# HGRN scores with the second half of the tokens reversed, so that keys of both halves share one stationary operand

## The chip, the core and the metric

The kernel runs on one core of a Trainium2 chip. The metric is the device time of one execution in microseconds (us). A core has a matrix engine (TensorE, PE in the rows, with PEld for its loads of the stationary operand), a vector engine (VectorE, DVE), an engine for activations and copies (ScalarE, ACT), GpSimd (POOL) and queues that start DMAs (SP for most). SBUF is the working memory with 128 partitions; PSUM takes the results of matmuls, in banks of 512 fp32 words per partition.

## The reference, cut to what matters

Four layers (HGRN2, mLSTM, S5, HGRN2), each followed by a SwiGLU block, over 256 tokens of width 1024. The change concerns the HGRN2 mixer of layers 0 and 3: 8 heads of 128 channels.

```python
q, f, v, g = split(x @ w_in, 4)
log_f = logaddexp(log(lb), log1p(-lb) + log_sigmoid(f))
k = (1 - lb) * sigmoid(-f);  q = silu(q)
# per head, with b = cumsum(log_f) along the tokens:
att[t, s] = sum_d q[t, d] * k[s, d] * exp(b[t, d] - b[s, d])     # for s <= t, else 0
o[t] = sum_s att[t, s] * v[s]
# the reference does this in chunks of 64 tokens with a carried state
o = rmsnorm_per_head(o) * silu(g);  return o @ w_out
```

The decay between key s and query t is a product of the gates of all tokens after s up to t, one for each channel.

## The kernel before

**Scores.** The 256 tokens are two halves of 128. Everything in the scores lies with the channels on the 128 partitions and the tokens along them. Heads are worked in pairs; a pair's keys `k`, gates `f` and queries `q` hold four blocks of 128 tokens in the order head 0 half 0, head 0 half 1, head 1 half 0, head 1 half 1. `hgrn_scores` builds `att` (keys on partitions, queries along) for a pair by doubling: at level m (1, 2, 4, ... 64) the queries in the right m of each 2m tokens meet the keys in the left m. Keys and queries are multiplied in place by products of gates, level by level (L604, L606), so that the product of a key and a query at level m already has its decay; `e` holds the products of gates of whole runs and is halved at each level (L613). The keys of half 0 with the queries of half 1 come last, as `cross` (L617).

**Matmuls of a pair.** The diagonal product (L574) streams 192 columns for each of the four blocks: 128 queries, and 64 queries already times their gate, which serve level 1. Identity and a mask pick the wanted entries into `att` (L576, L577). At levels 2 to 16 ACT gathers the left runs of keys and the right runs of queries of a block into one tile `kq` (L587, L588); PE takes all 128 columns of it as the stationary operand and streams its 64 queries (L590), one matmul for each block; a masked copy puts the result into `att` (L592). At levels 32 and 64 PE reads keys and queries directly, in blocks of m by m (L597), and ACT copies the result (L598).

**Order.** `scores` (L511) runs two pairs at once, level by level, and puts matmuls of other steps between (`query`, `pieces` of v and g, `heads_out`). The order on each engine is planned when the kernel is built: an instruction whose inputs are expected late is passed by a later one, but on the chip every engine keeps its planned order. Matmuls with weights are made of three fp32r products (`mm3`), with the weight in two parts that ACT (L123) and DVE (L124) make from each staged MB.

**Other names.** `pair_proj` (L467) makes gates or queries of one pair with 2 x 8 x 3 = 48 matmuls of 256 columns by `ws_block` (L157). `norm` and `put_split` (L198, L229) write the next layer's input, transposed, as two parts `xh` and `xl`; `head_turn` (L390) does that for the heads' output. The masks come from DRAM by one POOL DMA in each HGRN layer (L434).

```python
for i in range(4):                                        # L589, levels 2 to 16
    nc.tensor.matmul(pl[:, i * 64 : (i + 1) * 64], kq[:, i], split(kq, m)[:, i, :, 1], start=True, stop=True)
```

Of the kernel before, what the change touches and what calls it, by code (L numbers as in the profile page):

```python
# [28 lines left out]
LEVELS = (64, 32, 16, 8, 4, 2, 1)  # L29
# [5 lines left out]
class Trunk:  # L35
# [162 lines left out]
    def norm(self, h, banks, gb, last=None, perm=False):  # L198
# [18 lines left out]
        for n in range(4):  # L217
# [8 lines left out]
            self.put_split(pt[:, o : o + 256], 2 * n, h, perm=perm)  # L226
        self.x[h] = z

    def put_split(self, pt, k0, h, scale=None, perm=False, to=None):  # L229
# [3 lines left out]
        src = pt.rearrange("p (k t) -> p k t", k=n)  # L233
        t = slice(h * P, (h + 1) * P)
# [12 lines left out]
    def ffn(self, i, gb, out=None, perm=False, extra=()):  # L247
        nc, tc = self.nc, self.tc
        with tc.tile_pool(name=self.uid("ffn"), bufs=2, reuse_waits="tile") as fp:
# [112 lines left out]
            for h in range(2):  # L362
                self.layernorm(h, down[h], gb, out, perm)
# [26 lines left out]
    def head_turn(self, src, n, h, scale, ot):  # L390
# [4 lines left out]
        self.put_split(pt, 4 * n, h, scale, to=ot)  # L395
# [31 lines left out]
    def hgrn(self, j, gb, lb=None):  # L427
        nc, tc = self.nc, self.tc
        nw = self.const.tile([P, 1], F32, name=f"hnw{j}")
        nc.gpsimd.dma_start(nw, self.a["hg_nw"][j])  # L430
        with tc.tile_pool(name=self.uid("hg"), bufs=1, reuse_waits="tile") as hp, \
                tc.tile_pool(name=self.uid("hw"), bufs=2, reuse_waits="tile") as wp:
            msk = hp.tile([P, 5, 64], F32, name=self.uid("msk"))
# [33 lines left out]
            def pair_proj(st, tag="g"):  # L467
                us = self.wstage("w_hg", j, st)
                ps = self.bank(tag)
                for e in range(2):  # L470
                    self.ws_block(ps[:, e * 256 : (e + 1) * 256], us[e])
                return ps

            def heads_out(n):
# [3 lines left out]
                for h in range(2):  # L478
                    for e in range(4):
# [4 lines left out]
                        nc.tensor.matmul(o, att[:, 2 * (hd % 2) + h, :], v[:, h, c], start=True, stop=h == 0)  # L484
# [6 lines left out]
                for h in range(2):  # L491
                    on[n, h] = wp.tile([P, 768], F32, tag="q", name=self.uid("on"), bufs=4)[:, 0:512]
# [3 lines left out]
            def turn(n, h):  # L496
                o, gate = on[n, h], g[:, h, n * 512 : (n + 1) * 512]
                nc.vector.tensor_tensor(o, o, gate, ALU.mult)
                self.head_turn(o, n, h, nw, ot)
# [3 lines left out]
            def query(pr):  # L503
                pq = pair_proj(4 + pr, "a")
                q[pr] = wp.tile([P, 4, 192], F32, tag="q", name=self.uid("q"), bufs=4)
                self.act(q[pr][:, :, 0:P], pq.rearrange("p (a t) -> p a t", a=4), AF.Silu)
# [32 lines left out]
    def hgrn_gates(self, wp, pr, pf, lb):  # L539
# [11 lines left out]
        if lb is not None:  # L551
            for i in range(2):
                hd, s = slice(2 * pr + i, 2 * pr + i + 1), slice(i * 256, (i + 1) * 256)
                act(f[:, s], f[:, s], AF.Identity, scale=lb[:, 1, hd], bias=lb[:, 0, hd])
                act(k[:, s], k[:, s], AF.Copy, scale=lb[:, 1, hd])
        return k, f

    def hgrn_scores(self, wp, q, k, f, msk):
# [3 lines left out]

        nc = self.nc
        mul = lambda o, x, y: nc.vector.tensor_tensor(o, x, y, ALU.mult)
        att = wp.tile([P, 512], F32, tag="att", name=self.uid("att"), bufs=3).rearrange("p (a t) -> p a t", a=4)
        kt = k.rearrange("p (a t) -> p a t", a=4)
        qt = q[:, :, 0:P]
        e = f.rearrange("p (a n) -> p a n", a=4)
        split = lambda t, m: t.rearrange("p a (n s m) -> p a n s m", s=2, m=m)
# [9 lines left out]
        ends = wp.tile([P, 256], F32, tag="ends", name=self.uid("ends"))  # L579
        spare = 0  # L580
        for m in (1, 2, 4, 8, 16, 32, 64):
            n = P // (2 * m)
            if m > 1:
                pl = self.bank("a")
                if m < 32:
                    kq = wp.tile([P, 4, P], F32, tag="kq", name=self.uid("kq"))
                    nc.scalar.copy(split(kq, m)[:, :, :, 0], split(kt, m)[:, :, :, 0])  # L587
                    nc.scalar.copy(split(kq, m)[:, :, :, 1], split(qt, m)[:, :, :, 1])  # L588
                    for i in range(4):  # L589
                        nc.tensor.matmul(pl[:, i * 64 : (i + 1) * 64], kq[:, i], split(kq, m)[:, i, :, 1], start=True, stop=True)  # L590
                    mk = msk[:, 5 - m.bit_length(), :].bitcast(I32).rearrange("p (n m) -> p n m", m=m)
                    nc.vector.copy_predicated(split(att, m)[:, :, :, 1], mk[:, None].broadcast_to([P, 4, n, m]),  # L592
                                              pl[:, 0:256].rearrange("p (a n m) -> p a n m", a=4, m=m))
                else:
                    for lo in range(0, P, 2 * m):
                        for i in range(4):
                            nc.tensor.matmul(pl[lo : lo + m, i * m : (i + 1) * m], kt[:, i, lo : lo + m], qt[:, i, lo + m : lo + 2 * m], start=True, stop=True)  # L597
                        nc.scalar.copy(att[lo : lo + m, :, lo + m : lo + 2 * m], pl[lo : lo + m, 0 : 4 * m].rearrange("p (a t) -> p a t", a=4))  # L598
            ee = e.rearrange("p a (n s) -> p a n s", s=2)
            mine = slice(0, 4) if m < 64 else slice(0, 4, 2)  # L600
            his = slice(0, 4) if m < 64 else slice(1, 4, 2)
            b = lambda x, r: x[..., None].broadcast_to([P, len(range(4)[r]), n, m])
            x = split(kt, m)[:, mine, :, 0]
            mul(x, x, b(ee[:, mine, :, 1], mine))  # L604
            x = split(qt, m)[:, his, :, 1]
            mul(x, x, b(ee[:, his, :, 0], his))  # L606
            if m < 64:
                if m == 1:
                    new = ends
                else:  # L610
                    new, spare = f[:, spare : spare + 4 * n], spare + 4 * n
                e = new.rearrange("p (a n) -> p a n", a=4)
                mul(e, ee[:, :, :, 0], ee[:, :, :, 1])  # L613
            yield
        pc = self.bank("a")
        for i in range(2):
            nc.tensor.matmul(pc[:, i * P : (i + 1) * P], kt[:, 2 * i], qt[:, 2 * i + 1], start=True, stop=True)  # L617
        cross = wp.tile([P, 2, P], F32, tag="cross", name=self.uid("cross"), bufs=3)
        nc.scalar.copy(cross, pc[:, 0:256].rearrange("p (a t) -> p a t", a=2))
        yield att, cross  # L620
# [581 lines left out]
def trunk(tc, aps, out, layers=range(DEPTH), ffn=True):  # L1202
    with ExitStack() as ctx:
# [4 lines left out]
        perm0 = layers[0] == 2  # L1208
        with tc.tile_pool(name="first", bufs=1, reuse_waits="tile") as fp:
            src = fp.tile([P, KD, S], F32, name="xt")  # L1210
            t.warm_up(fp)
            for k in (slice(0, 2), slice(2, 4), slice(4, KD)):
                nc.sync.dma_start(src[:, k], aps["xt"][:, k])
                y, dh, dl = src[:, k], t.xh[:, k], t.xl[:, k]
                if perm0:
                    y = y.rearrange("p k (h c j) -> p k h j c", h=2, j=4)
                    dh, dl = (x.rearrange("p k (h j c) -> p k h j c", h=2, j=4) for x in (dh, dl))
                for h in (slice(0, 1), slice(1, 2)) if perm0 else (slice(0, S),):
# [127 lines left out]
```

## Time and profile before

| | before |
|---|---|
| median of 3 runs | 1317.61 us (1316.46 to 1317.88) |
| the profiled execution | 1319.75 us |
| its span, first to last instruction | 1317.9 us |
| PE busy | 1295.8 us, 98% |
| DVE busy | 968.3 us, 73% |
| ACT busy | 713.7 us, 54% |
| mean granted clock of PE | 0.994 |

A page of the profile gives busy times, the span in slices, the chain of work that ended last and groups of instructions by line. Views by window, by form, by line, of waits and in order of time go into it more closely. Records of matmuls overlap, and their ends are modelled, so the distance from one start to the next is a better measure than a record's duration. An fp32 matmul leaves two records, an fp32r one a single record. [...]

### The profile page before, as it was taken

The numbers are of one execution on the slowest core, as the hardware profiler recorded it, in microseconds if no ns is written. First come the engines' busy times: TensorE is split into PE (matmuls) and PEld (weight loads), VectorE is DVE, ScalarE is ACT, GpSimd is POOL, SyncE is SP. The second block draws the span as 40 slices with busy tenths as digits, with TensorE's granted clock in tenths as the row PEclk, the third lists the DMA queues.
The fourth block names the chain that finished last, engine by engine and source line by source line (L and its number), as shares of the span: only waits on it lengthen the run. The fifth ranks groups of instructions, "written<-read, shape, count | busy, mean of one in ns | idle before, by whom it ended". The sixth has DMA issues, their size and how long they took to land.

```text
span 1317.9 us, 19258 instructions
## 1 busy us (share of the span) xinstructions
PE 1295.8 (98%) x7430; PEld 1094.3 (83%) x7430; DVE 968.3 (73%) x1680; ACT 713.7 (54%) x1146; POOL 52.3 (4%) x75
## 2 busy tenths in 40 slices
PE   8999999999999999999998999999999999999997
PEld 6998888888788878888877778888879888888885
DVE  5877789776687699768489877666585886866664
ACT  5744475665556655657442355555459554555550
POOL 0000100000100110000010000000010001000001
PEclk8999999999999999999999999999999999999999
DMA  7732276657364257756567647555555312755540
GB/s 286 264 139 99 92 259 221 243 190 268 125 255 158 98 176 258 237 207 226 190 239 264 235 155 258 180 183 185 187 199 190 130 64 99 285 177 182 188 157 32
DMA packets 46123, 249.78 MB, mean 190 GB/s; under 512 B 5344, under 2 KB 9456, under 8 KB 19664
## 3 DMA queue, kind: packets, MB, share of 16 engines
q1 hardware_dynamic: 45712, 248.08, 52.7%
q8 instruction: 58, 0.95, 0.3%
q0 software_dynamic: 320, 0.48, 0.1%
q14 instruction: 33, 0.27, 0.1%
HBM read 234.91 MB, written 13.63 MB: 189 GB/s over the span
## 4 chain that ended last, share of the span: by engine, by line
PE 92%; DVE 3%; ACT 2%; DMA 1%; issue 1%; POOL 0%; SPq 0%; POOLq 0%; DVEq 0%; ACTq 0%
PE g L169 17%; PE g L140 10%; PE g L141 10%; PE g L142 10%; PE g L172 9%; PE a L140 8%; PE a L141 8%; PE a L142 8%; PE a L590 2%; PE t L1092 1%; PE t L224 1%; PE g L1080 1%; PE a L597 1%; PE a L574 1%; PE t L983 1%
## 5 line engine op out<-in xcount | busy, mean ns | idle before, releaser
L124 DVE TENSOR_TENSOR lo<-w,hi 128x1024 fp32r<-128x1024 f32 (+1 forms) x394 | 477.0, 1218 | 138.9 <-ACT hi L123 129.9
L123 ACT CAST hi<-w 128x1024 fp32r<-128x1024 f32 (+1 forms) x394 | 411.3, 1048 | 196.6 <-PE a L141 111.3
L169 PE MATMUL g<-xx,hi 128*128 128x512 f32 x1024 | 358.5, 395 | 0.2 <-DVE sum L301 0.2
L172 PE MATMUL g<-xx,lo 128*128 128x256 f32 x1024 | 267.4, 281 | 0.0
L169 PEld LDWEIGHTS g<-xx,hi 128*128 128x128 f32 x1024 | 186.7, 188 | 34.7 <-DVE sum L301 0.5
L172 PEld LDWEIGHTS g<-xx,lo 128*128 128x128 f32 x1024 | 192.4, 188 | 10.4
L140 PE MATMUL g<-hi,xx 128*128 128x512 f32 x424 | 172.8, 409 | 5.7 <-ACT hi L123 3.1
L141 PE MATMUL g<-hi,xx 128*128 128x512 f32 x424 | 170.3, 402 | 0.0
L142 PE MATMUL g<-lo,xx 128*128 128x512 f32 x424 | 169.1, 401 | 0.0
L140 PE MATMUL a<-hi,hh 128*128 128x512 f32 x344 | 135.8, 397 | 0.0
L141 PE MATMUL a<-hi,hl 128*128 128x512 f32 x344 | 135.7, 395 | 0.0
L142 PE MATMUL a<-lo,hh 128*128 128x512 f32 x344 | 135.3, 393 | 0.0
L300 ACT COPY sum<-g 128x256 f32<-128x256 f32 x128 | 47.7, 372 | 145.6 <-PE g L169 145.4
L301 DVE TENSOR_TENSOR sum<-g,sum 128x256 f32<-128x256 f32 x128 | 54.2, 424 | 71.6 <-ACT sum L300 71.2
L140 PEld LDWEIGHTS g<-hi,xx 128*128 128x128 f32 x424 | 80.4, 190 | 24.7 <-ACT xx L240 3.9
L142 PEld LDWEIGHTS g<-lo,xx 128*128 128x128 f32 x424 | 80.4, 190 | 18.3 <-DVE lo L124 0.9
L141 PEld LDWEIGHTS g<-hi,xx 128*128 128x128 f32 x424 | 80.5, 190 | 16.0 <-issue 0.2
L141 PEld LDWEIGHTS a<-hi,hl 128*128 128x128 f32 x344 | 64.8, 188 | 14.9 <-DVE hl L290 0.5
L142 PEld LDWEIGHTS a<-lo,hh 128*128 128x128 f32 x344 | 64.7, 188 | 14.8
L140 PEld LDWEIGHTS a<-hi,hh 128*128 128x128 f32 x344 | 64.4, 188 | 13.6 <-ACT hh L289 0.6
L140 PE MATMUL g<-xx,hi 128*128 128x256 f32 x200 | 56.8, 284 | 0.0
L142 PE MATMUL g<-xx,hi 128*128 128x256 f32 x200 | 56.5, 282 | 0.0
(304 smaller groups left out, 1874.8 us busy)
## 6 DMA issues: line engine op xcount, KB each, us to landing
w<-in_w_gu SPq DMA_DIRECT2D x88, 1024.0 KB, 4.9
w<-in_w_dn SPq DMA_DIRECT2D x44, 1024.0 KB, 4.9
w<-in_w_hg SPq DMA_DIRECT2D x30, 1024.0 KB, 5.0
w<-in_w_ml SPq DMA_DIRECT2D x12, 1024.0 KB, 5.0
gb<-in_ln SPq DMA_DIRECT2D x8, 1024.0 KB, 4.8
w<-in_w_ho SPq DMA_DIRECT2D x8, 1024.0 KB, 4.9
w<-in_w_so SPq DMA_DIRECT2D x8, 1024.0 KB, 6.1
ct<-s5ct SPq DMA_DIRECT2D x8, 768.0 KB, 9.3
```

The lines of the kernel that those rows point to most:

```text
L123: nc.scalar.copy(hi[:, c], part[:, c])
L124: nc.vector.tensor_tensor(lo[:, c], part[:, c], hi[:, c].bitcast(F32), ALU.subtract)
L140: mm(ps, lh, rh, start=start, stop=False)
L141: mm(ps, ll, rh, start=False, stop=False)
L142: mm(ps, lh, rl, start=False, stop=stop)
L169: whole = lambda: mm(ps, hi[:, c], self.xx[:, k].rearrange("p i t -> p (i t)"), start=k == 0, stop=k == KD - 1)
L172: mm(ps[:, S:], lo[:, c], self.xh[:, k], start=False, stop=False)
L224: nc.tensor.transpose(pt[:, (k % 4) * P : (k % 4 + 1) * P], z[:, k * P : (k + 1) * P], self.ident)
L300: nc.scalar.copy(t, ps[:, S:])
L301: nc.vector.tensor_tensor(t, ps[:, 0:S], t, ALU.add)
L574: nc.tensor.matmul(pd[:, i, :], kt[:, 2 * y + i], q[:, 2 * y + i, :], start=True, stop=True)
L590: nc.tensor.matmul(pl[:, i * 64 : (i + 1) * 64], kq[:, i], split(kq, m)[:, i, :, 1], start=True, stop=True)
```

## The change

The second half of the tokens is kept in reverse order wherever HGRN sees it: in the transposed input (written so by the host for layer 0, by `norm` and `put_split` for layer 3), hence in `q`, `k`, `f`, `v`, `g` and the scores. In a reversed half the keys of a level lie in the right m of each 2m tokens and the queries in the left m. So the keys of half 0 at level m and those of half 1 fill different places of the same 128 columns: ACT gathers them, one head at a time, into `kk`, and one matmul with 128 stationary key columns streams the 64 queries of half 0 and the 64 of half 1, straight from `q`. All levels from 1 to 64 do this; masks pick the entries for levels 1 to 32, and ACT copies them for level 64. The blocks of a pair are now ordered half, head, token; `ws_block` writes its PSUM result in that order, in two runs of 128. `head_turn` turns the second half back. The masks grow from 5 x 64 to 6 x 256 words per partition. The removed `perm0` branch isn't taken by this kernel.

```diff
     def ws_block(self, ps, unit):
         hi, lo = unit
+        xh, xl = (x if len(ps.shape) == 2 else x.rearrange("p k (h t) -> p k h t", h=2) for x in (self.xh, self.xl))
...
-            self.mm3(ps, (hi[:, c], lo[:, c]), (self.xh[:, k, :], self.xl[:, k, :]), k == 0, k == KD - 1)
+            self.mm3(ps, (hi[:, c], lo[:, c]), (xh[:, k], xl[:, k]), k == 0, k == KD - 1)
...
-    def put_split(self, pt, k0, h, scale=None, perm=False, to=None):
+    def put_split(self, pt, k0, h, scale=None, perm=False, to=None, rev=False):
...
+        if rev:
+            src = src[:, :, ::-1]
...
-                    self.ws_block(ps[:, e * 256 : (e + 1) * 256], us[e])
+                    self.ws_block(ps.rearrange("p (h a t) -> p a h t", h=2, a=2)[:, e], us[e])
...
+        keys = lambda t, m: view(t, 0, (256 + m, 2), (2 * m, P // m), (1, m))
+        queries = lambda t, m: view(t, m, (256 - m, 2), (2 * m, P // m), (1, m))
+        whose = lambda e, m, s: view(e, s, (2 * P // m + 1 - 2 * s, 2), (2, P // m), (0, m))
...
-        mul(q[:, :, P:], e[:, :, 1::2], qt[:, :, 1::2])
-        for y in range(2):
-            pd = self.bank("a")[:, 0:384].rearrange("p (a t) -> p a t", a=2)
-            for i in range(2):
-                nc.tensor.matmul(pd[:, i, :], kt[:, 2 * y + i], q[:, 2 * y + i, :], start=True, stop=True)
-            ay = att[:, 2 * y : 2 * y + 2, :]
-            nc.vector.tensor_tensor(ay, pd[:, :, 0:P], self.ident[:, None, :].broadcast_to([P, 2, P]), ALU.mult)
-            nc.vector.copy_predicated(ay[:, :, 1::2], msk[:, 4, :].bitcast(I32)[:, None].broadcast_to([P, 2, 64]), pd[:, :, P:])
-        mul(qt, qt, e)
+        pd = self.bank("a")
+        for i in range(4):
+            nc.tensor.matmul(pd[:, i * P : (i + 1) * P], k4[:, i], q4[:, i], start=True, stop=True)
+        nc.vector.tensor_tensor(a4, four(pd), self.ident[:, None, :].broadcast_to([P, 4, P]), ALU.mult)
+        mul(q, q, f)
...
-            if m > 1:
-                pl = self.bank("a")
-                if m < 32:
-                    kq = wp.tile([P, 4, P], F32, tag="kq", name=self.uid("kq"))
-                    nc.scalar.copy(split(kq, m)[:, :, :, 0], split(kt, m)[:, :, :, 0])
-                    nc.scalar.copy(split(kq, m)[:, :, :, 1], split(qt, m)[:, :, :, 1])
-                    for i in range(4):
-                        nc.tensor.matmul(pl[:, i * 64 : (i + 1) * 64], kq[:, i], split(kq, m)[:, i, :, 1], start=True, stop=True)
...
+            pl = self.bank("a")[:, 0:256]
+            kk = wp.tile([P, 2 * P], F32, tag="kk", name=self.uid("kk"))
+            nc.scalar.copy(view(kk, 0, (m, 2), (2 * m, 2 * n), (1, m)), keys(k, m))
+            for i in range(2):
+                nc.tensor.matmul(pl.rearrange("p (h a t) -> p a h t", h=2, a=2)[:, i], kk[:, i * P : (i + 1) * P],
+                                 view(q, i * P + m, (256 - m, 2), (2 * m, n), (1, m)), start=True, stop=True)
             if m < 64:
...
+                nc.vector.copy_predicated(queries(att, m), three(i32(msk[:, MASKED.index(m)])), three(pl))
+                for x, s in ((keys(k, m), 1), (queries(q, m), 0)):
+                    mul(x, x, whose(e, m, s))
...
+            else:
+                for h in range(2):
+                    s = slice(h * m, (h + 1) * m)
+                    nc.scalar.copy(a4[s, 2 * h : 2 * h + 2, m - h * m : P - h * m], pl[s, h * P : (h + 1) * P].rearrange("p (a t) -> p a t", a=2))
...
-        "xt": x.T.reshape(KD, P, S).transpose(1, 0, 2),
+        "xt": np.concatenate([x[:P], x[P:][::-1]]).T.reshape(KD, P, S).transpose(1, 0, 2),
```

## Rows read from the trace of the kernel before

**Rows 1.** The profile's page: busy time of PE, and the chain that ended last by engine
```profile
PE 1295.8 (98%) x7430; PEld 1094.3 (83%) x7430; DVE 968.3 (73%) x1680; ACT 713.7 (54%) x1146; POOL 52.3 (4%) x75
PE 92%; DVE 3%; ACT 2%; DMA 1%; issue 1%; POOL 0%; SPq 0%; POOLq 0%; DVEq 0%; ACTq 0%
```

**Rows 2.** Windows: length, busy us (instructions) by engine, PEclk, DMA share, GB/s
```profile
56.80:92.00 35.20, 35.20 (x274) 31.65 (x273) 28.26 (x69) 17.74 (x35) 0.00 (x0) 1.00 0.33 121
92.00:128.70 36.70, 36.36 (x246) 31.02 (x246) 29.63 (x70) 18.28 (x37) 1.86 (x2) 1.00 0.27 94
1020.00:1054.20 34.20, 34.17 (x266) 30.71 (x266) 29.57 (x70) 18.28 (x35) 0.00 (x0) 1.00 0.39 141
1054.20:1090.00 35.80, 35.40 (x245) 30.27 (x244) 29.32 (x71) 18.37 (x38) 1.84 (x2) 1.00 0.22 77
```

**Rows 3.** Timeline of PE, first layer: start us, us, engine, line, tiles, shapes, count
```profile
56.80 2.88 PE L574 MATMUL a<-q,k 128*128 128x192 f32 x16
59.38 0.53 PE L140 MATMUL g<-hi,xx 128*128 128x512 f32 x1
...
71.66 1.89 PE L590 MATMUL a<-kq 128*128 128x64 f32 x16
73.36 0.48 PE L141 MATMUL g<-hi,xx 128*128 128x512 f32 x1
...
83.51 0.69 PE L597 MATMUL a<-q,k 128*32 128x32 f32 x16
84.13 0.50 PE L141 MATMUL g<-hi,xx 128*128 128x512 f32 x1
...
87.56 0.68 PE L597 MATMUL a<-q,k 128*64 128x64 f32 x8
88.17 0.49 PE L141 MATMUL g<-hi,xx 128*128 128x512 f32 x1
...
98.25 0.38 PE L484 MATMUL a<-v,att 128*128 128x128 f32 x2
...
99.95 0.48 PE L142 MATMUL g<-lo,xx 128*128 128x512 f32 x1
```

**Rows 4.** Groups by form, 55 to 137 us: xcount | busy us, mean ns | idle
```profile
L592 DVE COPY_PREDICATED att<-msk,a 128x256 f32<-128x256 int32 x16 | 8.2, 512 | 5.2 <-PE a L590 5.1
...
L587 ACT COPY kq<-k 128x256 f32<-128x256 f32 x16 | 6.6, 411 | 5.7 <-DVE k L564 4.0 <-PE a L590 0.9 <-ACT kq L588 0.8
...
L576 DVE TENSOR_TENSOR att<-a,ident 128x256 f32<-128x256 f32 x8 | 3.1, 422 | 2.3 <-PE a L574 2.3
...
L577 DVE COPY_PREDICATED att<-msk,a 128x128 f32<-128x128 int32 x8 | 3.0, 454 | 0.0
...
L564 DVE TENSOR_TENSOR q<-f,q 128x256 f32<-128x256 f32 x3 | 1.3, 420 | 1.2 <-ACT q L90 1.2
```

**Rows 5.** Waits, 56 to 137 us: us in total, times, longest
```profile
DVE att L592 <- PE a L590: 5.1, 10, 1.4
```

**Rows 6.** Line 240's own view: ns min/median/max, first and last start, forms
```profile
L240 ACT CAST xx<-t x56: 358/372/381, 154.7 to 1134.2; 128x256 fp32r<-128x256 f32 x56
```

**Rows 7.** Timeline at the mask's first load
```profile
14.52 0.54 POOL L434 DMA_DIRECT2D msk<-in_c_lvl  x1 [11.40 <-DMA w<-in_w_hg]
...
16.94 2.00 ACT L123 CAST hi<-w 128x1024 fp32r<-128x1024 f32 x2 [1.44 <-DMA w<-in_w_hg]
```

**Rows 8.** Windows: the same columns as Rows 2, 10 to 20 us
```profile
10.00:20.00 10.00, 10.00 (x36) 7.93 (x35) 7.54 (x8) 6.71 (x7) 0.54 (x1) 0.77 0.97 380
```

**Rows 9.** Timeline of PE: projections of gates, then the mLSTM mask product
```profile
22.33 0.28 PE L140 MATMUL g<-xx,hi 128*128 128x256 f32 x1
22.45 0.28 PE L141 MATMUL g<-xx,lo 128*128 128x256 f32 x1
...
410.58 0.28 PE L717 MATMUL a<-mskb,idb 128*128 128x256 bf16 x1
410.79 0.70 PE L722 MATMUL a<-qk 64*128 64x256 f32 x2
```

More of the change, by code (lines that the diff above doesn't have):

```diff
@@ L28 @@
 HEAD_EPS = 1e-6
-LEVELS = (64, 32, 16, 8, 4, 2, 1)
+MASKED = (1, 2, 4, 8, 16, 32)
 BIG = 1e30
@@ L196, in layernorm, with norm @@
             self.norm(*args, **kw)
-    def norm(self, h, banks, gb, last=None, perm=False):
+    def norm(self, h, banks, gb, last=None, perm=False, rev=False):
         nc = self.nc
@@ L244, in put_split, with ffn @@
             nc.vector.scalar_tensor_tensor(ol, src, scale, oh.bitcast(F32), ALU.mult, ALU.subtract)
-    def ffn(self, i, gb, out=None, perm=False, extra=()):
+    def ffn(self, i, gb, out=None, perm=False, rev=False, extra=()):
         nc, tc = self.nc, self.tc
@@ L362, in ffn @@
             for h in range(2):
-                self.layernorm(h, down[h], gb, out, perm)
+                self.layernorm(h, down[h], gb, out, perm, rev)
     def transposed(self, pool):
@@ L432, in hgrn @@
                 tc.tile_pool(name=self.uid("hw"), bufs=2, reuse_waits="tile") as wp:
-            msk = hp.tile([P, 5, 64], F32, name=self.uid("msk"))
+            msk = hp.tile([P, len(MASKED), 256], F32, name=self.uid("msk"))
             nc.gpsimd.dma_start(msk, self.a["c_lvl"])
@@ L483, in heads_out @@
                         o = po[h][:, e * P : (e + 1) * P]
-                        nc.tensor.matmul(o, att[:, 2 * (hd % 2) + h, :], v[:, h, c], start=True, stop=h == 0)
+                        nc.tensor.matmul(o, att[:, 2 * h + hd % 2, :], v[:, h, c], start=True, stop=h == 0)
                         if h:
@@ L616, in hgrn_scores @@
         for i in range(2):
-            nc.tensor.matmul(pc[:, i * P : (i + 1) * P], kt[:, 2 * i], qt[:, 2 * i + 1], start=True, stop=True)
+            nc.tensor.matmul(pc[:, i * P : (i + 1) * P], k4[:, i], q4[:, 2 + i], start=True, stop=True)
         cross = wp.tile([P, 2, P], F32, tag="cross", name=self.uid("cross"), bufs=3)
         nc.scalar.copy(cross, pc[:, 0:256].rearrange("p (a t) -> p a t", a=2))
-        yield att, cross
+        yield a4, cross
     def mlstm(self, gb, after=None):
@@ L1214, in trunk @@
                 y, dh, dl = src[:, k], t.xh[:, k], t.xl[:, k]
[L1215 to L1218, printed above, removed]
-                    nc.scalar.copy(dh[:, :, h], y[:, :, h])
-                    nc.vector.tensor_tensor(dl[:, :, h], y[:, :, h], dh[:, :, h].bitcast(F32), ALU.subtract)
+                nc.scalar.copy(dh, y)
+                nc.vector.tensor_tensor(dl, y, dh.bitcast(F32), ALU.subtract)
                 if t.staged == 0:
@@ L1248, in trunk @@
                     spans = t.s5_prepare()
-                nxt = layers[layers.index(i) + 1 :][:1] == [2]
+                nxt = i + 1 if i < layers[-1] else None
                 with tc.tile_pool(name=t.uid("s5prep"), bufs=1, reuse_waits="tile") as t.s5pool:
-                    t.ffn(i, lambda: t.load_gb(2 * i + 1), out if i == layers[-1] else None, perm=nxt, extra=spans.pop(0) if spans else ())
+                    t.ffn(i, lambda: t.load_gb(2 * i + 1), out if i == layers[-1] else None, perm=nxt == 2, rev=nxt == 3, extra=spans.pop(0) if spans else ())
         if not ffn:
@@ L1277, in consts @@
     lvl = []
-    for m in LEVELS[2:]:
-        t = (c // m) * 2 * m + m + c % m
-        lvl.append((s // (2 * m) == t // (2 * m)) & ((s // m) % 2 == 0))
+    for m in MASKED:
+        t = (c // m) * 2 * m + c % m
+        same = s // (2 * m) == t // (2 * m)
+        lvl.append(np.concatenate([same & ((s // m) % 2 == h) for h in (0, 0, 1, 1)], 1))
     t = np.arange(P)[None, :]
```

63 lines of the change are left out of this document (25 added, 38 removed).

## Prediction

> **What bounds the kernel now.** I read the page first: TensorE (PE) is busy 98% of the span, and the chain of work that ended last is PE for 92% [rows 1]. So what counts is PE time, and a change on another engine counts only where it makes PE wait. I then found the four stretches in which attention scores are made (two pairs of heads at a time, in two HGRN layers) and read the table of windows for them [rows 2]. [...] The vector engine (DVE) is busy in 28.3 to 29.6 us of 34.2 to 36.7, that is 80 to 86%, so it is second, and not by much. ACT is at half.
>
> A busy PE says little by itself, because the records overlap and their ends are modelled. So I priced matmuls by the distance between starts in the order of time [rows 3]. An fp32 matmul leaves two records. With 192 columns streamed, 16 records go from 56.80 to 59.38: 0.161 us each. With 64 columns against a 128x128 stationary operand, 16 records go from 71.66 to 73.36: 0.106. With 128 columns (the outputs of the heads), 16 records go from 98.25 to 99.95: also 0.106. This is the row on which the change rests: streaming 64 columns costs as much as streaming 128. The 32-wide blocks cost 0.62 us for 16 records, the 64-wide ones 0.61 for 8.
>
> **PE, before and after, for one pair of heads.** Before: the diagonal product is 4 matmuls of 192 columns, 8 x 0.161 = 1.29; levels 2, 4, 8 and 16 are 4 matmuls of 64 columns each, 32 x 0.106 = 3.39; level 32 is 0.62, level 64 is 0.61; the cross block is 2 matmuls, 4 x 0.106 = 0.42. Sum 6.33 us. After: the diagonal product has 128 columns, 8 x 0.106 = 0.85; seven levels (1 is now one of its own) have 2 matmuls of 128 columns each, 28 x 0.106 = 2.97; cross 0.42. Sum 4.24 us. That is 2.09 less, and over 8 pairs **16.7 us** less on PE, if PE stays the bound.
>
> Two things in that price are not shown by the trace. The new matmuls stream queries with gaps from the tile itself: at level 1 every second word. The nearest row is level 4 of the old form (the 16 records at 71.66), which streams runs of 4 words with gaps, but only 64 columns. So a record of 128 gapped columns costs between 0.106 (no effect of gaps) and 0.212 (64 columns already at the limit, so twice that). I take 0.106: it is also the price of 128 columns without gaps, and 192 columns cost 0.161, hardly more by column, so the 64 columns seem held up by what goes with each record and not by the stream. Below 0.106 I see nothing, since the plain 128-column row stands there. Second, results are now written to PSUM in two runs (64 words each in a level; 128 each in the projections for queries and gates). The projections are 8 pair projections x 48 matmuls x 2 layers = 768, now 0.12 us from start to start [rows 9]. The nearest row with two runs is the mLSTM mask product of 256 columns: from its start to the next one 0.21 us pass, but the next matmul also begins with its own load there. So two runs cost between 0 and 0.09 us more. I take 0, since the run breaks once in 256 columns and the neighbour's load explains the distance.
>
> [...]
>
> **DVE, for one pair.** Groups by form [rows 4]: away go the product of gates and queries for level 1 (0.42), two identity products (2 x 0.42) and two masked copies of 128 columns (2 x 0.45). Added are one identity product of 512 columns (at most the 0.84 of the two that it replaces), one masked copy for level 1 and one for level 32 (0.51 each). The products with the decays keep their 256 elements and their number. Net: -0.42 - 0.90 + 1.02 = -0.30 us, or 0.6 less in a stretch of two pairs. So DVE stays at 114.4 us over the four stretches (116.8 now) while PE falls from 141.9 us of stretch to 125.2. DVE would then be busy 91% of the time, against 82% now and 86% in the best stretch. That is where I expect part of the gain to stay.
>
> **ACT and the waits that it adds.** Eight copies of mixed keys and queries of 0.41 us [rows 4] become seven of keys alone; the two small copies of level 32 go, the one of level 64 becomes two. ACT gains time and isn't the bound. But levels 1, 32 and 64 now need such a copy before their matmul, where before PE read the tiles directly. Behind that matmul in PE's queue stand the weight matmuls that fill the stretch; if nothing else covered it, 3 copies x 8 pairs x 0.41 = 9.8 us. What covers it is the other pair of the stretch and the filling matmuls (a level is followed at once by a weight matmul [rows 3]). The level 1 copy needs only the gates, so it is early. Queries, now streamed in place, may be multiplied only after PE has read them; the masked copy ahead in DVE's queue waits for the same matmul already (5.1 us of such waits in the first layer [rows 5]), so nothing new is late.
>
> **The rest.** The mask grows from 160 KB to 768 KB, twice. Its first load starts at 14.52 on the POOL queue, while DMA runs at 380 GB/s [rows 8]: 0.62 MB more are 1.6 us. ACT is then waiting for weights; it ends their casts at 18.94 and PE first streams against them at 22.33 [rows 7, 9]. That 3.4 us is the cover; gone, it costs 1.6 us once. I take 0 for both loads; the second, uncovered, would cost 1.6 us again. The reversed writes replace straight ones of the same size. The permuted copies for S5, in the same group as the plain ones, all lie between 358 and 381 ns [rows 6], so I take 0 for 8 ACT and 8 DVE copies; at twice their time the ACT ones would cost 3 us. The reversal of the input is done outside, no step on the chip. The gate scaling of the second layer keeps its sizes.
>
> **Sum.** Upper end of the gain: 16.7 us, PE price alone. Lower end, if DVE can't be filled above the best share that a stretch shows: 29.57 / 34.20 = 0.865, so 114.4 / 0.865 = 132.3 us for the four, a gain of 9.6. I take the middle, **13.2 us**, because both engines would sit close to their totals, and two queues that feed each other seven times in a row don't both run full. The profiled execution took 1319.75 us (span 1317.9 and 1.85 around it), so 1306.5 in its terms; it is 2.1 us above the median of the three runs, and against that median of 1317.61 the forecast is **1304.4 us**.
>
> **Rivals.**
> *The vector engine becomes the bound.* For it: 80 to 86% busy now and no work taken away to speak of. Against it: it waits 5.1 us in the first layer for just those matmuls that get shorter [rows 5]. With its share of today, 0.823, the stretches take 139.0 us, a gain of 2.9: 1314.7. Between the best and the mean share: 1308 to 1314.7.
> *Gapped streaming (slower).* Place: the 28 records of a pair's levels. A pair breaks even with the old form where 1.27 + 28r = 6.33, r = 0.181 us. At the bound 0.212 it takes 7.21, 0.88 more, 7.0 us over 8 pairs: 1324.6. Against it: 0.106 is also the price of 128 plain columns, so no row shows that the gaps set it.
> *Two-run results (slower too).* The gain is eaten at 13.2 / 768 = 17 ns for one projection matmul; at 30 ns they cost 23 us and the kernel takes about 1327; at the bound of 0.09 us nearly 70 us more than forecast. Against it: 128 contiguous words in each run. [...]
> *It doesn't pay.* The new order of PE's queue puts levels where their keys aren't copied yet, the 9.8 us of copies and the mask's 1.6 come out uncovered, and the time stays where it was: 1315 to 1320.
>
> **Chances.** Forecast (1300.5 to 1308) 0.58; vector bound (1308 to 1315) 0.23; nothing gained 0.08; gapped streaming 0.05; two-run results 0.06. The range is 1300.5 to 1315, which leaves out the last three. About 0.2% (2.6 us) is what a measurement can tell from no change. Faster by more: 0.81; within it: 0.08; slower: 0.11.
>
> **What the profile after would show.** Right: level matmuls of 128 columns at 0.106 us from record to record at all levels; four stretches some 13 us shorter in sum; DVE near 90% there; projections still 0.12 apart. Wrong: level records above 0.18 (gaps), projections above 0.135 (two runs), PE waiting at the level's weight load for the copy of keys in more than a few places, or stretches whose DVE share isn't over 0.865 although PE has less to do.

## The result, and the profile after

| | before | after |
|---|---|---|
| median | 1317.62 us (1316.46 to 1317.88, 4 runs) | **1304.58 us** (1304.39 to 1305.97, 4 runs) |
| ratio to before | | 0.9904 [0.9891, 0.9917] |
| the profiled execution | 1319.75 us | 1304.51 us |
| its span | 1317.9 us | 1302.6 us |
| mean granted clock of PE | 0.994 | 0.995 |

The kernel is 13.0 us faster; 1304.4 had been forecast. The page of after, first its busy times, then its chain by engine (they answer to [rows 1]):

```profile
PE 1278.9 (98%) x7206; PEld 1077.1 (83%) x7206; DVE 965.8 (74%) x1664; ACT 709.5 (54%) x1130; POOL 52.3 (4%) x75
PE 91%; DVE 5%; ACT 2%; issue 1%; DMA 1%; POOL 0%; POOLq 0%; SPq 0%; DVEq 0%; ACTq 0%
```

PE is busy 16.9 us less, DVE 2.5 (2.4 were forecast). In the chain DVE's share has gone from 3% to 5%: some PE time has become time in which PE stands, that is, waits idle, behind DVE. The windows of the four score stretches in after (columns as in [rows 2]) say where:

```profile
55.77:88.65 32.88, 32.73 (x227) 29.01 (x226) 27.73 (x64) 17.16 (x33) 0.00 (x0) 1.00 0.42 150
88.65:120.60 31.95, 30.59 (x181) 25.28 (x180) 28.26 (x66) 15.99 (x30) 1.86 (x2) 1.00 0.21 74
1011.34:1042.47 31.13, 30.89 (x218) 27.81 (x219) 28.86 (x65) 17.62 (x33) 0.00 (x0) 1.00 0.36 128
1042.47:1074.50 32.03, 30.68 (x181) 25.31 (x180) 28.30 (x67) 16.15 (x31) 1.84 (x2) 1.00 0.27 98
```

They sum to 128.0 us, from 141.9; DVE is busy 113.2 us of them, 0.88. But PE is no longer full in the second stretch of each layer: 30.6 of 32.0 us. Both of these stretches have POOL work in them. And in the first stretch of layer 3 PE is full (30.89 of 31.13 us) while DVE is busy 28.86 us, a share of 0.93.

A cleaner measure than the stretches, whose ends I chose, is the **score stage**: from the first score matmul of an HGRN layer to the first matmul of its output projection. From the timelines it takes 79.92 us (layer 0) and 77.91 (layer 3) before, and 73.17 and 71.44 after: 6.75 + 6.47 = **13.2 us**, the size of the whole gain. Of the 15.2 us between the two profiled executions the other 2 lie outside: layer 0's first score matmul starts at 55.77 instead of 56.80 (in the first 20 us the granted clock was 0.91 on average in after and 0.83 before), and several later parts are some tenths shorter.

The timeline of PE in after, at the first diagonal product and level 1 (L583, L594), then at the level that follows the first heads' outputs:

```profile
55.42 0.28 PE L140 MATMUL a<-xx,hi 128*128 128x256 f32 x1
55.54 0.28 PE L141 MATMUL a<-xx,lo 128*128 128x256 f32 x1
...
55.77 1.05 PE L583 MATMUL a<-q,k 128*128 128x128 f32 x8
56.58 0.48 PE L140 MATMUL g<-hi,xx 128*128 128x512 f32 x1
...
58.30 0.64 PE L594 MATMUL a<-q,kk 128*128 128x128 f32 x4
58.77 1.05 PE L583 MATMUL a<-q,k 128*128 128x128 f32 x8
...
102.08 0.40 PE L141 MATMUL g<-hi,xx 128*128 128x512 f32 x1
103.60 0.68 PE L594 MATMUL a<-q,kk 128*128 128x128 f32 x4 [1.12 <-DVE q L572]
104.03 0.48 PE L142 MATMUL g<-lo,xx 128*128 128x512 f32 x1
```

Eight records of the diagonal product take 0.81 us, 0.101 each; four of level 1, which streams every second word, 0.47, or 0.118 with the change to the next kind of matmul; four of a later level 0.43, or 0.108. So a record of 128 gapped columns costs what one of 64 columns cost [rows 3]. A projection written in two runs of 128 still starts 0.12 after the one before it [rows 9]. And one stand of 1.12 us is new, before the level at 103.60, with DVE named as its releaser. Here are DVE and POOL at that time:

```profile
99.09 0.66 DVE L494 TENSOR_REDUCE ss<-t 128x4 f32<-128x512 f32 x1
99.66 0.73 DVE L598 COPY_PREDICATED att<-msk,a 128x256 f32<-128x256 int32 x1
101.83 1.29 DVE L499 TENSOR_TENSOR on<-a,rs 128x512 f32<-128x512 f32 x2 [1.43 <-POOL rs L183]
103.03 0.42 DVE L572 TENSOR_TENSOR q<-q,ends 128x256 f32<-128x256 f32 x1
```

```profile
99.85 0.20 POOL L182 TENSOR_SCALAR rs<-ss 128x8 f32<-128x8 f32 x1 [84.94 <-DVE ss L494]
100.13 1.67 POOL L183 TENSOR_TENSOR rs<-rs,root 128x8 f32<-128x8 f32 x1
```

`heads_out(0)` sums squares on DVE, POOL raises 128 x 8 sums to the power -0.5 in 1.67 us, and DVE then scales the heads (L499). While POOL works, DVE stands 1.43 us, since the scaling is next in its planned order; the product with decays that the next level of the scores needs (103.03) is queued behind it. PE runs out of weight matmuls at 102.5. Layer 3 has the same stand of PE, 1.10 us at 1057.48. The kernel before had the same stand of DVE and almost none of PE, as its timelines of DVE and PE show:

```profile
104.36 1.29 DVE L494 TENSOR_TENSOR on<-a,rs 128x512 f32<-128x512 f32 x2 [1.44 <-POOL rs L182]
```

```profile
106.84 1.10 PE L590 MATMUL a<-kq 128*128 128x64 f32 x8 [0.20 <-ACT kq L588]
```

### The profile page after: what moved, and what is told of

Same layout as the page of the kernel before. It is cut to its first block, busy times and chain, and to the rows that moved or that the text cites. A ratio compares the mean times of both kernels' runs of the same rounds, so it can differ in the third digit from the quotient of the medians.

```text
span 1302.6 us, 18792 instructions
## 1 busy us (share of the span) xinstructions
PE 1278.9 (98%) x7206; PEld 1077.1 (83%) x7206; DVE 965.8 (74%) x1664; ACT 709.5 (54%) x1130; POOL 52.3 (4%) x75
## 4 chain that ended last, share of the span: by engine, by line
PE 91%; DVE 5%; ACT 2%; issue 1%; DMA 1%; POOL 0%; POOLq 0%; SPq 0%; DVEq 0%; ACTq 0%
PE g L170 18%; PE g L140 10%; PE g L142 9%; PE g L141 9%; PE g L173 9%; PE a L140 8%; PE a L141 8%; PE a L142 8%; PE a L594 1%; PE t L1091 1%; DVE lo L124 1%; PE t L225 1%; PE g L1079 1%; DVE att L598 1%; PE t L982 1%
## 5 line engine op out<-in xcount | busy, mean ns | idle before, releaser
L124 DVE TENSOR_TENSOR lo<-w,hi 128x1024 fp32r<-128x1024 f32 (+1 forms) x394 | 476.9, 1219 | 141.2 <-ACT hi L123 132.5
L173 PE MATMUL g<-xx,lo 128*128 128x256 f32 x1024 | 267.4, 281 | 0.0
L140 PE MATMUL g<-xx,hi 128*128 128x256 f32 x200 | 56.5, 283 | 0.0
L141 PE MATMUL g<-xx,lo 128*128 128x256 f32 x200 | 56.4, 282 | 0.0
```

The costliest lines, as they stand in the source:

```text
L124: nc.vector.tensor_tensor(lo[:, c], part[:, c], hi[:, c].bitcast(F32), ALU.subtract)
L140: mm(ps, lh, rh, start=start, stop=False)
L141: mm(ps, ll, rh, start=False, stop=False)
L173: mm(ps[:, S:], lo[:, c], self.xh[:, k], start=False, stop=False)
```

## Experiments

Each was timed beside the kernel before on the same chip, in three groups; its medians there were 1317.14, 1318.78 and 1318.10 us. The names in code type are those that the table of S5 below uses.

**The same kernel again** (`same_again`). No edit.

> The changed kernel itself, unchanged, beside the other three. Expected 1304 to 1305 us. It gives the spread between executions of one program, above all in the stretch of S5 (from its first matmul to the first matmul of the following feed-forward block), which has so far been between 118.8 and 121.9 us in programs that have the same S5 code. If that spread is one of executions and not of programs, this run shows another value than 120.21 us there, with the granted clock of PE below 1.00 in another place or for another time, and the same 73.2 and 71.4 us in the two score stages.

1304.80 us (1303.36 to 1305.81), ratio 0.989 [0.9874, 0.9907]. Score stages 73.08 and 71.49 us, within 0.1 of the first profile; S5 120.76, 0.55 longer. So the score stage repeats well, and S5, the state-space layer, less so (below).

**Each half's queries in a matmul of their own** (`split64`).

```diff
-                nc.tensor.matmul(pl.rearrange("p (h a t) -> p a h t", h=2, a=2)[:, i], kk[:, i * P : (i + 1) * P],
-                                 view(q, i * P + m, (256 - m, 2), (2 * m, n), (1, m)), start=True, stop=True)
+                for h in range(2):
+                    nc.tensor.matmul(pl[:, (2 * h + i) * 64 : (2 * h + i + 1) * 64], kk[:, i * P : (i + 1) * P],
+                                     view(q, i * P + m + h * (256 - m), (2 * m, n), (1, m)), start=True, stop=True)
```

> The changed kernel with one edit undone: each half's 64 queries are streamed by a matmul of their own against the same shared keys, so a level has 4 matmuls of 64 columns again; keys, masks, copies and results stay. Theory (a record costs 0.112 us whether it streams 64 or 128 columns): 28 more records for a pair, 8 pairs, 28 x 8 x 0.112 = 25 us more than the changed kernel's 1304.6, so about 1329, slower than the kernel before. Rival (the gain came from what shares no column: the copies, the level 32 and 64 blocks, the removed columns): a record of 64 columns costs half, and the time stays near 1305.

1324.33 us (1321.89 to 1326.7), ratio 1.0058 [1.0037, 1.008]. Its timeline of PE:

```profile
71.04 1.89 PE L595 MATMUL a<-q,kk 128*128 128x64 f32 x16
72.74 0.48 PE L141 MATMUL g<-hi,xx 128*128 128x512 f32 x1
...
73.29 1.00 PE L595 MATMUL a<-q,kk 128*128 128x64 f32 x8
74.10 0.47 PE L140 MATMUL g<-hi,xx 128*128 128x512 f32 x1
```

16 records of 64 columns take 1.70 us, as in [rows 3]; 8 take 0.81, as the 8 of 128 columns in after. The stages are 83.00 and 81.22 us, 19.6 longer in sum. 28 records more in each of 8 pairs, at 0.112 (the median distance of level records), would be 25 us. From start to start in the two traces the level records take 23.0 us more (0.102 for each one added); PE's stands are 1.1 us shorter, and the matmuls in between 2.5, which leaves the 19.6. So for 64 and 128 columns the record is what costs, not its columns: the median is 0.112 us for both (see below).

**Results to every second word of PSUM** (`gap_out`).

```diff
-                nc.tensor.matmul(pl.rearrange("p (h a t) -> p a h t", h=2, a=2)[:, i], kk[:, i * P : (i + 1) * P],
+                nc.tensor.matmul(pl.rearrange("p (h t a) -> p a h t", h=2, a=2)[:, i], kk[:, i * P : (i + 1) * P],
```

> The changed kernel, but the level matmuls write every second word of PSUM (head and token interleaved) and not runs of 64; what is read back is then in a mixed order, so the scores are not the reference's. Theory: the fp32 records stay at 0.112 us, time within 1 us of the changed kernel's 1304.6. [...]

1304.13 us (1303.44 to 1305.89), ratio 0.9903 [0.9887, 0.992]; stages 73.07 and 71.47 us, 0.1 less in sum than in after. In its timeline of PE four records of level 1 again take 0.47 us:

```profile
58.80 0.64 PE L594 MATMUL a<-q,kk 128*128 128x128 f32 x4
59.27 1.05 PE L583 MATMUL a<-q,k 128*128 128x128 f32 x8
```

For fp32 matmuls of this size non-contiguous results cost nothing here. Only level matmuls were written so; for the fp32r projections there are just the runs of 128.

**No wait for POOL's root** in the first half's heads (`no_root`).

```diff
+        self.unit = c.tile([P, 8], F32, name="unit")
+        self.nc.gpsimd.memset(self.unit, 1.0)
...
-                r = self.rsqrt(ss.rearrange("p a b -> p (a b)"), 8, HEAD_EPS, 1.0 / P)
+                r = self.rsqrt(ss.rearrange("p a b -> p (a b)"), 8, HEAD_EPS, 1.0 / P) if n else self.unit
```

> The changed kernel without the wait for the norm's root in the first half of the heads: heads 0 to 3 are scaled by 1 and not by their root (the root is left out there, and the sum it would use is still made). Theory (what the gain lacks to 16.7 us is mostly PE standing once per layer at a level whose queries DVE has not multiplied, since DVE itself stands 1.4 us before the scaling that waits for POOL's root): both stands of 1.1 to 1.3 us go, 2.2 to 2.6 us less than 1304.6, about 1302.2. Rival (DVE's share sets the limit): DVE's work is the same, time stays within 0.5 us of 1304.6.

1300.46 us (1299.24 to 1302.65), ratio 0.9879 [0.9862, 0.9896]. Stages 71.46 and 69.95 us, 3.2 less in sum; the stand before the level is gone and none over 0.4 us is left. That settles the place of most of the loss, but not yet that the order on DVE is at fault, since the edit takes the wait away altogether. (The total fell by more; S5 was 1.3 us shorter in its profile, see below.)

**The scaling one level later**, with all its work (`late_scale`, `late_again`).

```diff
-                for h in range(2):
-                    on[n, h] = wp.tile([P, 512], F32, tag="q", name=self.uid("on"), bufs=4)
...
+                def scale():
+                    for h in range(2):
+                        on[n, h] = wp.tile([P, 512], F32, tag="q", name=self.uid("on"), bufs=4)
...
+                return scale
...
-            scores((2, 3), ([lambda: heads_out(0)], g0[0:1], g0[1:2], g0[2:3], g0[3:], g1[0:1], g1[1:2], g1[2:3]))
+            late = []
+            scores((2, 3), ([lambda: late.append(heads_out(0))], g0[0:1] + [lambda: late[0]()], g0[1:2], g0[2:3], g0[3:], g1[0:1], g1[1:2], g1[2:3]))
...
-            heads_out(1)
+            heads_out(1)()
```

> The changed kernel with the scaling of the first four heads' outputs issued one level later in the program, behind the second pair group's next level, so that DVE has level work to do while POOL makes the root; all results the same. Theory: the two stands of PE go, 2 us less than 1304.6, about 1302.5. Rival 1 (DVE's share): no change beyond 0.5 us. Rival 2 (the outputs hold two of the four PSUM banks longer and the levels lack them): 1 to 3 us slower than 1304.6.

> The scaling of the first half's head outputs is issued one level later, as in late_scale, and nothing else. Theory: the two score stages take 71.8 and 70.2 us again, 2.6 us less than in the changed kernel, and what was missing of that in the earlier total lies in the stretch of S5. Then the total is between 1301.5 (S5 as in the changed kernel) and 1303.5 us (S5 long again). Rival: a later scaling makes S5 longer by itself, by a changed order of transfers; then S5 takes 121 to 122 us again at a lower clock, and the total is 1303.4.

1303.44 us both times (1303.25 to 1303.72, and 1300.34 to 1304.46); ratios 0.99 [0.9885, 0.9915] and 0.988 [0.9862, 0.9897]. The stages are 71.77 and 70.22 us, then 71.82 and 70.26: 2.6 and 2.5 us less than in after, as expected. The window of the second run over the second stretch of layer 0, and DVE's timeline there:

```profile
88.20:119.00 30.80, 30.56 (x181) 25.29 (x180) 28.37 (x67) 16.02 (x30) 1.87 (x2) 1.00 0.23 78
```

```profile
100.55 0.47 DVE L577 TENSOR_TENSOR q<-q,ends 128x256 f32<-128x256 f32 x1
101.32 1.29 DVE L501 TENSOR_TENSOR on<-a,rs 128x512 f32<-128x512 f32 x2 [0.29 <-POOL rs L183]
```

The products of the scores now run while POOL works, and DVE's wait is 0.29 us instead of 1.43. DVE is busy 92% of this stretch and PE 99%: the two do run full together. But the total fell by 1.1 to 1.4 us only, which the intervals of the ratios don't tell from after. S5 took 121.87 and 121.83 us, so the rival in the second expectation was right on the length; its reason, other transfers, is dealt with below.

**Less work for DVE, the same for PE** (`no_low`, `no_low2`). The first also took one of the eight buffers for low parts; the diff is that of the second.

```diff
-            lo = self.split.tile([P, 1024], F32R, tag="lo", name=self.uid("lo"))
+            if not (name == "w_hg" and at[-1] in (2, 3, 12, 13, 14, 15)):
+                lo = self.split.tile([P, 1024], F32R, tag="lo", name=self.uid("lo"))
...
                     nc.scalar.copy(hi[:, c], part[:, c])
+                    if name == "w_hg" and at[-1] in (2, 3, 12, 13, 14, 15):
+                        lo = hi
+                        continue
                     nc.vector.tensor_tensor(lo[:, c], part[:, c], hi[:, c].bitcast(F32), ALU.subtract)
```

> Left out: the low parts of six of the sixteen staged weight blocks of the HGRN input projection (of q and of g), which are zeros here; their matmuls run as before. That takes 12 subtractions of 1.22 us from DVE in each HGRN layer, 29 us in all, and nothing from PE. If the 3.5 us of PE gain that did not arrive are lost because DVE is nearly full (88% of the four stretches), most of them come back: 1301 to 1302 us. If they are lost in one stand behind GpSimd's root and small waits for copies, DVE's load matters little: the stand before the level after the heads' outputs stays at over 1 us, the stages lose at most 0.5 us each, and the total is 1303.5 to 1304.6.

> Left out: the subtraction that makes the low part of six of the sixteen weight blocks of the HGRN input projection (of q and of g); the matmuls read the high part in its place, so PE's work is the same. Unlike no_low it leaves all buffers as they are, of which the earlier run had one less throughout. DVE loses 29 us. If DVE's load holds the 3.5 us back, the stages shorten by 1 us or more each, and their stand behind the heads' outputs goes; if the stand behind GpSimd's root does, it stays at about 1.3 us and the stages shorten by 0 to 1 us.

The first took 1318.97 us (1315.37 to 1321.75), ratio 0.9999 [0.9987, 1.0011], far from both expectations. Layers without HGRN are longer too (mLSTM 96.24 us, from 93.24 in after, and its feed-forward block 188.21, from 186.44). What it differs in from the second is the buffer and a tile of zeros, and DVE stands 203.6 us in all just before making low parts (141.2 in after), so its total says nothing on DVE's load; its stages took 72.18 and 71.89 us. The second took 1305.10 us (1303.86 to 1306.12), ratio 0.9901 [0.9881, 0.992], with stages of 72.40 and 71.43 us. Its windows of layer 0, its PE and its DVE at the stand:

```profile
55.96:88.65 32.69, 32.61 (x228) 29.19 (x227) 18.99 (x56) 17.18 (x32) 0.00 (x0) 1.00 0.42 153
88.65:120.60 31.95, 30.52 (x182) 25.67 (x181) 28.30 (x66) 16.04 (x30) 1.87 (x2) 1.00 0.24 77
```

```profile
102.55 0.68 PE L598 MATMUL a<-q,kk 128*128 128x128 f32 x4 [1.35 <-DVE q L576]
```

```profile
100.78 1.29 DVE L503 TENSOR_TENSOR on<-a,rs 128x512 f32<-128x512 f32 x2 [1.43 <-POOL rs L187]
```

Over the four stretches DVE has 19.5 us less to do (93.7 us instead of 113.2), most of it in the first of each layer, where its share falls from 0.84 to 0.58. The stages are 0.8 us shorter in layer 0 and not at all in layer 3, against 2.6 us in sum for moving the scaling, and the stand is no shorter (1.35 us for 1.12). So in the first stretches, where PE is full anyway, less work for DVE brings little. In the second stretches, where PE falls short, this run takes next to nothing from DVE (28.30 us for 28.26 in layer 0, 27.36 for 28.30 in layer 3), so there it tests nothing. What shows for these that the order on DVE holds PE up, and not its load, is `late_again`: DVE has the same work there (28.37 us) and PE is full.

**More work for DVE** (`more_dve`).

```diff
+        self.junk = c.tile([P, 128], F32, name="junk")
+        self.nc.gpsimd.memset(self.junk, 0.0)
...
                 mul(new, e[:, 0::2], e[:, 1::2])
+                if 1 < m < 64:
+                    mul(self.junk, self.junk, self.junk)
```

> Added: one product of 128 x 128 on DVE at each of the levels 2 to 32, on a tile that nobody else uses: 5 x 8 pairs x 0.287 = 11.5 us of DVE time, which takes its share of the four stretches from 0.88 to 0.97 if they keep their length. If a share near 0.9 is as far as DVE can be filled, nearly all of it arrives: stages 5 us longer each, 1314 us or more. If DVE's 14.8 idle us can be used and single waits make the loss, less than half arrives: stages up to 2.8 us longer each, 1306 to 1310.

1306.04 us (1304.29 to 1306.48), stages 73.09 and 71.51. No verdict: the products depend on nothing, and the planner put all 40 at the start of the program, as this tile's own view shows (at its end the first and last start and the form), so DVE's share of the stretches stayed at 0.88.

```profile
L574 DVE TENSOR_TENSOR junk<-junk x40: 282/292/295, 2.3 to 34.9; 128x128 f32<-128x128 f32 x40
```

**Later scaling and four buffers for gathered keys** (`late_kk4`; the diff is that of the buffers alone).

```diff
-            kk = wp.tile([P, 2 * P], F32, tag="kk", name=self.uid("kk"))
+            kk = wp.tile([P, 2 * P], F32, tag="kk", name=self.uid("kk"), bufs=4)
```

> The scaling one level later, and four buffers instead of two for the gathered keys, so that ACT doesn't wait for PE to have read the level before (4.4 us of such waits in the first layer). If these waits are part of the 2.8 us of PE stands that remain in each score stage, the stages fall by 0.5 us or more below 71.8 and 70.2. If ACT's copy is early anyway, they stay within 0.2 us.

1302.12 us (1300.43 to 1303.63), ratio 0.9878 [0.9857, 0.99]; stages 71.71 and 69.86 us, 0.1 and 0.4 less than in late_again. The two rows of ACT's waits in layer 0, of late_again and then of this run:

```profile
ACT kk L597 <- DVE k L577: 5.0, 5, 1.7
ACT kk L597 <- PE a L599: 4.4, 3, 2.1
```

```profile
ACT kk L597 <- DVE k L577: 9.0, 9, 2.1
ACT kk L597 <- PE a L599: 0.9, 2, 0.6
```

ACT waits less for PE and that much longer for DVE: a wait that was there for two reasons. Layer 0 fits the second expectation, layer 3 lies between the two, and in total time the two runs can't be told apart.

**The S5 stretch.** It has the same instructions in all of these programs, and lasts (from its first matmul on the states, `g<-s5u,bm`, to the first of the next feed-forward block):

| | S5 stretch, us | lost to the clock, us |
|---|---|---|
| no_root / split64 | 118.95 / 118.81 | 1.7 / 1.7 |
| before / after / same_again | 120.35 / 120.21 / 120.76 | 3.4 each |
| gap_out / more_dve | 120.84 / 120.66 | 3.4 each |
| late_scale / late_again / late_kk4 / no_low2 | 121.87 / 121.83 / 122.02 / 122.02 | 5.1 each |

The second column is the sum over windows of 1 us of what the granted clock misses to 1.00. Less that column, every row is 116.7 to 117.4 us. (`no_low`, one buffer short, is left out: 123.14 us, 3.4 lost.) Some of these windows of after, around PE's second wait for DVE:

```profile
711.41:712.41 1.00, 0.00 (x0) 0.00 (x0) 1.00 (x2) 0.00 (x0) 0.00 (x0) 1.00 0.17 51
712.41:713.41 1.00, 0.00 (x0) 0.00 (x0) 1.00 (x4) 0.00 (x0) 0.00 (x0) 0.55 0.86 254
713.41:714.41 1.00, 0.83 (x8) 0.86 (x10) 0.96 (x4) 0.00 (x0) 0.00 (x0) 0.50 1.02 381
714.41:716.41 2.00, 2.00 (x23) 2.00 (x21) 1.97 (x5) 0.00 (x0) 0.00 (x0) 0.50 1.02 426
```

PE waits 2.2 us for DVE, to 713.58. About 1.1 us into the wait the clock falls to 0.50, and by windows of 1 us it stays there for 6.8 us, to 719.3: the last 5.8 us of that are PE's work. A wait of 2.1 us some 16 us earlier left it at 1.00 in after. If the loss comes from these two waits, then filling them should bring it back:

```diff
-            def inputs(b):
-                px = pxs[b] = self.bank("g")
+            def inputs(b, again=False):
+                px = pxs[b] = pxs[b] if again else self.bank("g")
...
                 elif b < 7:
                     inputs(b + 1)
+                    if b in (2, 4):
+                        inputs(b + 1, again=True)
```

(`fill`; `late_fill` has the later scaling too. `again` writes the same matmuls into the same place.)

> The changed kernel, with 8 of the S5 input matmuls issued twice into the same place at two points (16 records of 0.11 us, about 1.8 us each time). They come just ahead of PE's two waits of 2.1 and 2.2 us for DVE in the S5 stretch, so they should fill these waits and delay nothing. Theory: the granted clock falls to 0.50 after these stands, costing 3.4 us there in the changed kernel (1.7 us in some runs of other programs, 5.1 in others). Without the stands the clock stays at 1.00: S5 stretch 116.8 to 117.4 us instead of 120.2 to 120.8, total 1301.4. Rival: the lower clock has another cause, or comes anyway; then S5 stays at 120 to 121 us and the total at 1304.5 or above, by what of the 3.6 us of added matmuls isn't covered.

> Both edits: the scaling one level later, and the S5 input matmuls issued twice at the two waits. Theory: score stages 71.8 and 70.2 us (2.6 us less than in the changed kernel), S5 stretch 116.8 to 117.4 us; total 1298.4 to 1299.2. If the later scaling makes S5 longer by something other than the clock, S5 stays above 118 us and the total above 1300.

`fill`: **1302.18 us** (1301.73 to 1302.54), ratio 0.9879 [0.9861, 0.9897]. `late_fill`, both edits: **1298.36 us** (1297.95 to 1299.56), ratio 0.9851 [0.9829, 0.9874]. S5 takes 117.67 and 117.66 us, 0.3 above what was expected; the total of `fill` is 0.8 above its 1301.4, that of `late_fill` within 0.1 of the range given. By the intervals `late_fill` is clear of after; `fill` alone is not quite, and its S5 stretch is what shows the effect. Windows of 16 us that hold the two waits, in after, late_again and late_fill:

```profile
694.41:710.41 16.00, 13.45 (x109) 11.06 (x108) 15.14 (x26) 6.52 (x9) 0.00 (x0) 1.00 0.71 260
710.41:726.41 16.00, 13.38 (x96) 11.93 (x96) 13.25 (x24) 4.59 (x8) 0.00 (x0) 0.79 0.77 294
```

```profile
692.67:708.67 16.00, 13.45 (x97) 11.19 (x97) 13.60 (x23) 6.07 (x8) 0.00 (x0) 0.89 0.64 225
708.67:724.67 16.00, 13.38 (x100) 12.11 (x99) 13.16 (x25) 4.28 (x6) 0.00 (x0) 0.79 0.79 286
```

```profile
692.57:708.57 16.00, 15.23 (x125) 12.84 (x124) 15.13 (x26) 6.51 (x9) 0.00 (x0) 1.00 0.73 240
708.57:724.57 16.00, 14.98 (x124) 12.62 (x123) 15.72 (x29) 5.75 (x9) 0.00 (x0) 1.00 0.92 353
```

With both waits filled the clock stays at 1.00, and with the later scaling on top S5 is no longer than without it (117.66 us, 117.67). So the later scaling did not lengthen S5 by transfers; the clock's falls did (5.1 us lost, 3.4 in after). Why the clock falls after one wait and not after a like one stays open, and so does whether the later scaling makes falls likelier: the three programs with it and no filled waits all lost 5.1 us in the executions profiled, but so did `no_low2` without it. With both edits the kernel is 6.2 us below after, and that is the fastest version run.

## Why the prediction was right, point by point

**The price of a record: right.** It carries the whole gain, and `split64` shows it alone. At 0.106 a pair was to lose 2.09 us on PE. By distances in the traces (medians of 0.112 for 64 and for 128 columns and 0.163 for 192, means of 0.041 and 0.072 for the small blocks) a pair falls from 6.55 to 4.47: 2.08. Added up from start to start over both score stages, with stands of more than 0.15 us apart, the score matmuls take 50.8 us before and 33.7 after, 17.1 less. The 16.7 us stand.

**Gapped streaming and results in two runs, both taken as 0: right.** Level 1, with the widest gaps for its size, costs 0.47 us for four records and a later level 0.43 to 0.45; projections still stand 0.12 apart. `gap_out` went further than the change does: no two consecutive words of a level's result lie side by side in it, and its stages were 0.1 us shorter in sum than in after.

**The 13.2 us: right in size, wrong in its reason.** The step that failed is the middle between the PE price and a limit on DVE's share. DVE's work was forecast well: 113.2 us in the four stretches for 114.4, with the identity product at 0.69 us (at most 0.84 forecast). But the argument that two engines near their totals can't both run full was wrong: in after itself the first stretch of layer 3 ran with DVE at 93% and PE at 99%, and with the scaling moved the second stretch of layer 0 did so at 92% and 99%.

The sum from start to start says where the gain went: of the 17.1 us, 2.2 are lost to PE's stands (0.6 before, 2.8 after) and 1.7 to the matmuls between (106.5 and 108.2; a change between the two kinds counts on either side, so this split is rough), which leaves the 13.2. The stands are one in each layer, 1.12 and 1.10 us, behind a root on POOL that the prediction left out. With the scaling moved they are back at 0.5 us in sum, and 2.6 us of the stages with them. What the 1.7 us are isn't shown.

In the kernel before, the same wait of DVE was in the trace (1.44 us) with PE covered; the shorter levels bring PE to that place sooner. A question that [rows 2] raise would have found it: why is PE short of full only in the second stretch of each layer (36.36 of 36.70, 35.40 of 35.80), and why are POOL instructions in just these two? That the middle of two bounds came out at the measured size is luck.

**Copies for levels 1, 32 and 64, taken as covered: right.** One ACT copy a level gathers the keys of both heads, and PE itself stands 0.3 us in sum over both layers for these copies (`ACT kk L592`), against 9.8 uncovered. The weight loads wait for them more often than the few places allowed, seven times and 2.9 us in layer 0 (13 times and 5.2 us in both), but beside other matmuls. Some of the waits of after, 54 to 134 us (they answer to [rows 5]):

```profile
ACT kk L592 <- PE a L594: 4.4, 3, 2.1
DVE on L499 <- POOL rs L183: 3.5, 2, 2.1
PEld a L594 <- ACT kk L592: 2.9, 7, 0.6
DVE att L598 <- PE a L594: 1.1, 4, 0.5
```

DVE's waits for the levels' matmuls fell from 5.1 us to 1.1, as they would when PE gets faster at just these. **The mask** (1.6 us at most): after it ACT waits the same 1.44 us for weights as in [rows 7]:

```profile
16.81 2.00 ACT L123 CAST hi<-w 128x1024 fp32r<-128x1024 f32 x2 [1.44 <-DMA w<-in_w_hg]
```

**The reversed writes:** ACT's casts take 358, 373 and 380 ns (least, median, most) for 358, 372 and 381 in [rows 6]. Copies, mask and reversed writes were all taken as 0, rightly.

**The rivals.** A bound by DVE would have left the stretches at 139 us in sum and a share of 0.82; they came to 128.0 at 0.88. The two slower ones needed records above 0.181 us or projections 17 ns longer; neither is there.

## What to carry to other kernels

When work is taken from the bounding engine, don't take a share of another engine's busy time as the limit of the gain (here 93% of DVE went with 99% of PE): look in the trace of before for places where a third engine's slow instruction already makes an in-order queue stand (here 1.44 us of DVE behind POOL's root), and ask whether the bounding engine, arriving sooner, still has cover there. Where an instruction must wait for a slow result, issue what others need ahead of it. And compare programs by stages before by totals, since a stretch with the same instructions can move by 3 us for a reason of its own (here S5, 118.81 to 122.02 us).

## What the runs showed of the hardware that was not expected

- An fp32 matmul with a full stationary operand cost the same for 64 and 128 streamed columns (a median of 0.112 us from record to record, two records each), also with the columns read or the results written with gaps (0.47 us for four records of level 1, in after and in `gap_out`); 192 columns cost 0.163.
- With PE's waits of about 2.2 us in S5 the granted clock fell to 0.50 in some executions and places, and not in others with the same instructions; the loss in S5 was 1.7, 3.4 or 5.1 us, and S5's length went with it. Repeating 16 matmuls (at each wait 16 records, by an estimate from 0.112 us a record 1.8 us of PE time) whose results were already there kept the clock at 1.00 and S5 2.5 us shorter (117.67 against 120.21); the total was 2.4 to 2.6 us lower (1302.18 against 1304.58 and 1304.80).
- A root of 128 x 8 numbers by a power on POOL took 1.67 us; in order behind it DVE stood 1.43 us, and PE 1.12.
- One buffer less of eight for the low parts of weights came with 14 us on the whole program (1318.97 against 1305.10), with DVE standing 203.6 us just before making them (141.2 in after).
